# Activation buffers per channel tile, and a plain float32 second matmul in the attention of the last 512 queries

## The chip, the core and the metric

The kernel runs on one core of a Trainium2 chip. The metric is the device time of one execution in microseconds. Five engines matter here: PE (TensorE, matrix multiplication; PEld is its weight load), DVE (VectorE), ACT (ScalarE), POOL (GpSimd) and SP (SyncE, which here only issues DMAs). Each engine runs its own instructions in their order and waits on semaphores for the others. Matmuls write to PSUM, which DVE and ACT read; DMAs move data between memory and SBUF.

## What is computed

A trunk of two layers over 2048 positions of width 1024, all in float32: a gated short convolution, one K/V projection, then a stick-breaking attention with 8 heads of 64, and RMS norms before, between and behind them. Cut to what matters:

```
u = rmsnorm(x) @ w_in_a                       # 1024 -> 4 x 1024: B, C, h, G
x = x + ((B * conv3(C * h)) * silu(G)) @ w_out_a
k, v = split(rmsnorm(x) @ w_kv)               # 8 heads of 64
q, g = split(rmsnorm(x) @ w_in_b)
z = q k^T / 8                                 # strictly causal
rev = reverse cumulative sum over keys of log_sigmoid(-z)
o = exp(z + rev) @ v                          # masked entries are 0
x = x + (o * silu(g)) @ w_out_b
out = rmsnorm(x)
```

## The kernel before

**Layout.** Positions stand in reverse order on the free dimension, so that the cumulative sum over later keys becomes a running product from left to right. The 2048 positions are cut into four chunks of 512 (`c` = 0 to 3); the last, `c` = 3, is "the last 512 queries" and sees all four key chunks. Channels are cut into eight tiles of 128 (`k` = 0 to 7).

**Split operands.** Most matmuls are float32r, a reduced form of float32. To keep precision an operand is split into a high part (ACT's copy to float32r, line 173) and a low part (the source minus the high part, line 174, on DVE or POOL). A linear layer (`mm3`, lines 210 to 222) then takes three matmuls per channel tile: high x high, high x low, low x high.

**Buffers.** `act_tile` (line 115) is one tile of 32 KB per partition that holds the high and low parts of all eight channel tiles of one activation; there are two. They hold `h` (normed input), `y` (mixer output), `xn` (normed residual) and later `og` (gated attention output) in turn. `x1` and, at the end, `x2` share one tile of 16 KB with tag `og`. Weights are split once and kept in memory (`split_d`); their split tiles `whl` rotate through four buffers, the raw ones `wraw` through two. A buffer is given out again when all readers of its last tile are done.

**Folding.** `fold_gains` (line 361) multiplies the norm gains into `w_kv` and `w_in_b`, 16 tiles of 128x1024. Each is loaded to a `wraw` buffer, scaled on DVE (line 366), split into a `whl` buffer (lines 192 and 173 to 174) and stored (line 194). It runs beside the input projections of chunks 0 and 1.

**Attention.** For a head and a query chunk (`attention`, line 465) the key chunks are visited from the diagonal down. For each of four query blocks of 128: two matmuls for the scores `z` (lines 486, 487), two sigmoids on ACT (489, 491), a running product on DVE (500) whose last column is carried to the next key chunk, and a multiplication for the weights `w` (504). Then, for each of four key blocks (`kb` = 3 to 0): transposes of `w` on PE into PSUM tile `wt` (512), a split of `wt` into `wth` on ACT and `wtl` on DVE (519, that is 173 and 174), and two float32r matmuls (521, 522) that add `wth` and `wtl` times v to the accumulator `av`. The 128 columns of the v operand are the high and the low part of 64 channels, so half of the partitions of `av` holds v's high part and the other half its low part; lines 529 and 530 add the halves at the end of a head. On the diagonal, the blocks have 512, 384, 256 and 128 valid queries; the last is padded to 256.

**Order.** Generators yield estimated costs, and `merge` advances the stream that is furthest behind its share; the framework's own scheduler then settles each engine's order. In the last stage the first six heads of chunk 3 are merged with a fill: the rest of chunk 3's projections (`proj_rest`), and the output projections `out_b` and norms of chunks 0 to 2. Heads 6 and 7 are merged with the output projection of chunk 3 over its first 384 channels (`out_b_last`). There, every third matmul of the fill (`GRP`) is tied to follow an anchor, the second `av` matmul of the block `SLACK` = 8 anchors back (lines 217 to 219, 523). After the last head `out_b_last` adds the last 128 channels and writes the norm.

Of the kernel before, what the change touches and what calls it, by code (L numbers as in the profile page):

```python
# [14 lines left out]
P = 128  # L15
S = 2048
D = 1024
NH = 8
# [3 lines left out]
NR, NW, NT, NL, NWB, NRAW, NWTS = 5, 8, 4, 5, 4, 2, 2  # L22
# [8 lines left out]
GRP, GRY, SLACK = 3, 6, 8  # L31
# [14 lines left out]
def kernel(  # L46
# [49 lines left out]
    v_d = [dram.tile([P, 4, NH, 2, 64], F32, name=f"v_d_{c}") for c in range(NCH)]  # L96
    sg_d = [[dram.tile([P, CH], F32, name=f"sg_d_{c}_{h}") for h in range(NH // 2)] for c in range(NCH)]
# [17 lines left out]
    def act_tile(nm):  # L115
        return sb.tile([P, 2, KD, CH], F32R, name=nm, tag="act", bufs=2)
# [59 lines left out]
    def load_raw(src, nm, kt=KD):  # L176
        raw = sb.tile([P, kt, P], F32, name=f"wr_{nm}", tag="wraw", bufs=NRAW)
        if len(src.shape) == 2:
            src = src.rearrange("(k p) n -> p k n", p=P)
        nc.sync.dma_start(out=raw, in_=src)  # L180
        return raw

# [6 lines left out]
    def split_w(raw, key, nm, kt=KD, eng=nc.vector):  # L189

        wt = w_tile(nm, kt)
        split(wt[:, 0], wt[:, 1], raw, eng)
        split_d[key] = dram.tile([P, 2, kt, P], F32, name=f"sw_{nm}")
        nc.sync.dma_start(out=split_d[key], in_=wt.bitcast(F32))
        return wt

    def load_w(src, key, nm, kt=KD, eng=nc.vector):

        if key not in split_d:
            return split_w(load_raw(src, nm, kt), key, nm, kt, eng)  # L200
        wt = w_tile(nm, kt)
        nc.sync.dma_start(out=wt.bitcast(F32), in_=split_d[key])
        return wt
# [6 lines left out]
    def mm3(ps, wts, a, kt=KD):  # L210

        hi, lo = wts[:, 0], wts[:, 1]
        n = 0
        for k in range(kt):
            for w, m in ((hi, 0), (hi, 1), (lo, 0)):
                ins = nc.tensor.matmul(ps, w[:, k, :], a[:, m, k, :], start=n == 0, stop=n == 3 * kt - 1)  # L216
# [16 lines left out]
    def norm_x_late(c, between=None):  # L233

        hc = act_tile(f"h_{c}")
        xs = []
        for k in range(KD):
            if k == 1 and between is not None:
                between()
            tag, bufs = (("w", NW), ("R", NR) if k < NR else ("ld", NL))[c]  # L240
            x = sb.tile([P, CH], F32, name=f"xh_{c}_{k}", tag=tag, bufs=bufs)
            nc.sync.dma_start(out=x, in_=xT[k * P:(k + 1) * P, cols(c)])
            xs.append(x)
            ga = gains["a"][:, k:k + 1]
            nc.scalar.activation(hc[:, 0, k, :], x, AF.Copy, scale=ga)
            nc.vector.scalar_tensor_tensor(out=hc[:, 1, k, :], in0=x, scalar=ga, in1=hc[:, 0, k, :].bitcast(F32),
                                           op0=ALU.mult, op1=ALU.subtract)
        return hc, xs
# [26 lines left out]
    def norm_x(c):  # L275
        hc = act_tile(f"h_{c}")
        pb = bcast(rx[c], f"hb{c}")
        for k in range(KD):
            x = load_x(c, k, "n")
            nc.vector.scalar_tensor_tensor(out=x, in0=x, scalar=gains["a"][:, k:k + 1], in1=pb,  # L280
                                           op0=ALU.mult, op1=ALU.mult)
            split(hc[:, 0, k, :], hc[:, 1, k, :], x)
        return hc
# [88 lines left out]
    def proj_out(c):  # L372

        y = act_tile(f"y_{c}")
        for k in range(KD):
            t = ld512(f"yr_{c}_{k}")
            nc.sync.dma_start(out=t, in_=y_d[c][k])
            split(y[:, 0, k, :], y[:, 1, k, :], t, nc.gpsimd if k in YLP else nc.vector)
        acc = sb.tile([P, CH], F32, name=f"acc_x1{c}", tag="acc", bufs=2)
        yield 0.0  # L380
        for ob in range(KD):
            wts = load_w(w_out_a[0][:, ob * P:(ob + 1) * P], ("o", ob), f"o{c}_{ob}")
            ps = lin(f"po_{c}_{ob}")
            yield from mm3(ps, wts, y)
            if ob == 0:
                x1 = sb.tile([P, KD, CH], F32, name=f"x1_{c}", tag="og", bufs=1)
            x = x1[:, ob, :]
# [5 lines left out]
        xn = act_tile(f"xn_{c}")  # L393
        pb = rstd_bcast(acc, f"x1{c}")
        for k in range(KD):
            t = x1[:, k, :]
            nc.vector.tensor_mul(t, t, pb)
            split(xn[:, 0, k, :], xn[:, 1, k, :], t, nc.gpsimd if k in XNL else nc.vector)
        kept[c] = xn
        yield YP[c] * 24 * MM  # L400
# [21 lines left out]
    def proj_v(c, vb):  # L422
# [10 lines left out]
        nc.sync.dma_start(out=v_d[c][:, :, 2 * vb:2 * vb + 2, :, :], in_=vt.bitcast(F32))  # L433
        yield rest(24) + 2 * MM
# [30 lines left out]
    def attention(c, h, ot):  # L465
# [8 lines left out]
        for kc in range(c, -1, -1):  # L474
# [4 lines left out]
            vt = sb.tile([P, 4, 2, 64], F32R, name=f"vv_{nm}", tag="vv", bufs=2)  # L479
            nc.scalar.dma_start(out=vt.bitcast(F32), in_=v_d[kc][:, :, h, :, :])  # L480
# [26 lines left out]
            for kb in range(3, -1, -1):  # L507
# [5 lines left out]
                first, final = diag and kb == 3, kc == 0 and kb == 0  # L513
                wh = sb.tile([P, CH], F32R, name=f"wth_{nm}_{kb}", tag="wth", bufs=NWTS)
# [8 lines left out]
                anchors.append(ins)  # L523
# [18 lines left out]
    def og_tile(c):  # L542

        if c == 0:
            og_t[0] = sb.tile([P, 2, 4, CH], F32R, name="og_0", tag="og", bufs=1)
        elif c == 1:
            t = act_tile("og_12")
            og_t[1], og_t[2] = t[:, :, 0:4, :], t[:, :, 4:8, :]
        elif c == 3:
            t = act_tile("og_3")  # L550
            og_t[3] = t[:, 0].rearrange("p (m k) n -> p m k n", m=2)
            x2_t.append(sb.tile([P, KD, CH], F32, name="x2_3", tag="og", bufs=1))

    x2_t = []

    def gated(c, k, r=None):

        if c not in og_t:
            og_tile(c)
        og = og_t[c]  # L560
# [8 lines left out]
        split(og[:, 0, k, :], og[:, 1, k, :], r)  # L569
# [51 lines left out]
    def out_b_last(c):  # L621

        og, x2 = og_t[c], x2_t[0]
        for ob in range(KD):
# [4 lines left out]
            nc.sync.dma_start(out=x2[:, ob, :], in_=x1_d[c][ob])  # L629
            nc.vector.tensor_add(x2[:, ob, :], x2[:, ob, :], ps)  # L630
# [8 lines left out]
        for ob in range(KD):  # L639
            ps = lin(f"pol_{ob}")  # L640
            yield from mm3(ps, wl[ob // 4][:, :, ob % 4:ob % 4 + 1, :], og[:, :, 3:4, :], kt=1)
            nc.vector.tensor_add(x2[:, ob, :], x2[:, ob, :], ps)
            if ob < 2:
                nc.scalar.activation(acc[ob], x2[:, ob, :], AF.Square)
            else:
                sq = t512(f"sq_x2{c}{ob}")
                nc.scalar.activation(sq, x2[:, ob, :], AF.Square)
# [9 lines left out]
        for k in range(KD):  # L657
            if k in (1, 4, 7):
                nc.scalar.activation(x2[:, k, :], x2[:, k, :], AF.Copy, scale=gains["f"][:, k:k + 1])
                nc.gpsimd.tensor_mul(x2[:, k, :], x2[:, k, :], pbs)  # L660
            else:
                nc.vector.scalar_tensor_tensor(out=x2[:, k, :], in0=x2[:, k, :], scalar=gains["f"][:, k:k + 1],
                                               in1=pb, op0=ALU.mult, op1=ALU.mult)
            nc.sync.dma_start(out=outT[k * P:(k + 1) * P, cols(c)], in_=x2[:, k, :])
# [101 lines left out]
```

## Time and profile before

| | |
|---|---|
| Median of 3 runs | 1909.34 us (1906.65 to 1910.77) |
| The profiled execution | 1907.57 us, its span 1905.8 us |
| Mean granted TensorE clock in it | 0.977 |
| PE, DVE, ACT, POOL busy | 1784.0, 1264.6, 769.7, 436.2 us |
| Moved by DMA | 443.64 MB, 233 GB/s |
| Attention of chunk 3: first and last head end | 1527.2 and 1874.3 us |

How to read it: the span runs from the first to the last instruction of the profiled execution. A group's row gives line, engine, operation, output <- inputs, shape of array and operands, count, then busy time and mean of one in ns, then the idle time of the engine just before and who ended it. A matmul's duration is a latency; since matmuls are pipelined, two of them in a row start closer together than one lasts. A row of the table of stages gives a window in us and its length, then busy time and (count) of PE, PEld, DVE, ACT and POOL, the granted clock, the DMA share and GB/s.

### The profile page before, as it was taken

What the parts mean: (1) busy time and instruction counts of PE and PEld (TensorE: products, weight loads), DVE (VectorE), ACT (ScalarE), POOL (GpSimd) and SP (SyncE); (2) the same over time, 40 slices, a digit from 0 to 9 for tenths busy, and PEclk for the clock granted to TensorE, in tenths of its full rate; (3) what the DMA queues carried; (4) which work ended last, traced back from release to release, by engine and by line L of the source; (5) the groups of instructions that cost most, each with busy time, mean ns of one, the idle gap of its engine ahead of it and who ended that gap; (6) DMA issues with size and microseconds to landing.
All of it is one profiled execution on the core that took longest, in us unless ns stands there. A gap on an engine that the chain in (4) does not pass through costs nothing.

```text
span 1905.8 us, 24702 instructions
## 1 busy us (share of the span) xinstructions
PE 1784.0 (94%) x8312; PEld 1449.4 (76%) x8312; DVE 1264.6 (66%) x1895; ACT 769.7 (40%) x1481; POOL 436.2 (23%) x822
## 2 busy tenths in 40 slices
PE   7899999999999999999999999999979999878785
PEld 5787777778888888888788888888857788656563
DVE  7644554574334264428888346788897999999996
ACT  6312222241123133314545233444555666565553
POOL 5000000000011021103123112222422224654641
PEclk9999999999999999999999999999999999999897
DMA  9648787798887779776767776655746665877751
GB/s 314 210 150 248 248 254 237 243 312 304 295 284 270 258 237 286 246 262 224 242 211 268 238 253 219 202 175 197 258 144 196 197 199 193 284 225 250 252 177 50
DMA packets 226702, 443.64 MB, mean 233 GB/s; under 512 B 16912, under 2 KB 131600, under 8 KB 199952
## 3 DMA queue, kind: packets, MB, share of 16 engines
q1 hardware_dynamic: 166496, 383.30, 60.0%
q10 hardware_dynamic: 59920, 58.74, 10.9%
q8 instruction: 66, 1.08, 0.2%
q14 instruction: 60, 0.49, 0.1%
q0 software_dynamic: 160, 0.02, 0.1%
HBM read 314.34 MB, written 127.66 MB: 232 GB/s over the span
## 4 chain that ended last, share of the span: by engine, by line
PE 69%; DVE 14%; DMA 9%; issue 4%; ACT 2%; POOL 1%; SPq 0%; ACTq 0%; POOLq 0%; DVEq 0%
PE pX L216 8%; PE po L216 7%; PE pG L216 7%; PE pC L216 7%; PE pB L216 6%; PE pg L216 5%; PE pk L216 5%; PE pq L216 5%; PE pv L216 4%; PE wt L512 4%; DVE R L500 4%; PE av L522 3%; DVE w L504 2%; PE av L521 2%; PE z L486 2%
## 5 line engine op out<-in xcount | busy, mean ns | idle before, releaser
L500 DVE TENSOR_TENSOR_SCAN R<-R,R,ones 128x512 f32<-128x512 f32 x192 | 256.6, 1339 | 11.4 <-ACT R L489 11.1
L489 ACT ACTIVATE R<-z 128x512 f32<-128x512 f32 (+1 forms) x320 | 174.2, 544 | 173.1 <-DVE R L500 78.4
L174 DVE TENSOR_TENSOR wtl<-wt,wth 128x512 fp32r<-128x512 f32 (+1 forms) x320 | 185.6, 600 | 67.2 <-ACT wth L173 66.3
L504 DVE TENSOR_TENSOR w<-w,R 128x512 f32<-128x512 f32 (+1 forms) x320 | 212.2, 671 | 21.3 <-POOL R L499 3.0
L173 ACT CAST wth<-wt 128x512 fp32r<-128x512 f32 (+1 forms) x320 | 160.3, 526 | 160.1 <-PE wt L512 137.4
L216 PE MATMUL pC<-h,whl_C 128*128 128x512 f32 x768 | 197.1, 405 | 14.4 <-ACT whl_C L173 8.3
L216 PE MATMUL pG<-h,whl_G 128*128 128x512 f32 x768 | 186.6, 393 | 9.9 <-ACT whl_G L173 9.9
L499 POOL COPY R<-R 128x1 f32<-128x1 f32 x192 | 112.3, 585 | 360.8 <-DVE R L500 293.3
L216 PE MATMUL pX<-h,whl_X 128*128 128x512 f32 x768 | 187.6, 393 | 6.0 <-ACT cs L320 3.9
L216 PE MATMUL po<-y,whl_o 128*128 128x512 f32 x768 | 187.8, 394 | 2.0 <-DVE x L389 1.3
L512 PE MATMUL wt<-ident,w 128*128 128x128 f32 x1088 | 177.8, 278 | 9.2 <-DVE w L504 5.1
L216 PEld LDWEIGHTS pC<-h,whl_C 128*128 128x128 f32 x768 | 148.2, 195 | 49.4 <-ACT whl_C L173 8.3
L216 PE MATMUL pB<-h,whl_B 128*128 128x512 f32 x768 | 185.6, 392 | 0.0
L216 PEld LDWEIGHTS pG<-h,whl_G 128*128 128x128 f32 x768 | 143.2, 188 | 41.0 <-ACT whl_G L173 11.6
L491 ACT ACTIVATE w<-z 128x512 f32<-128x512 f32 (+1 forms) x320 | 172.7, 543 | 0.5 <-PE wt L512 0.5
L216 PEld LDWEIGHTS pX<-h,whl_X 128*128 128x128 f32 x768 | 142.2, 188 | 37.6 <-ACT cs L320 5.1
L216 PEld LDWEIGHTS po<-y,whl_o 128*128 128x128 f32 x768 | 144.2, 189 | 33.5 <-DVE x L389 1.9
L512 PEld LDWEIGHTS wt<-ident,w 128*128 128x128 f32 x1088 | 138.6, 143 | 38.3 <-DVE w L504 7.2
L216 PEld LDWEIGHTS pB<-h,whl_B 128*128 128x128 f32 x768 | 143.0, 188 | 30.1 <-DVE cv L356 0.4
L522 PE MATMUL av<-wtl,vv 128*128 128x512 f32 (+1 forms) x320 | 129.1, 405 | 36.7 <-DVE wtl L174 36.6
L500 DVE TENSOR_TENSOR_SCAN R<-R,ones 128x512 f32<-128x512 f32 (+3 forms) x128 | 116.1, 913 | 33.8 <-POOL R L495 32.2
L486 PE MATMUL z<-kt,q 128*128 128x512 f32 (+1 forms) x320 | 129.1, 405 | 4.1 <-ACT w L491 3.4
(170 smaller groups left out, 2655.3 us busy)
## 6 DMA issues: line engine op xcount, KB each, us to landing
whl_o<-sw_o SPq DMA_DIRECT2D x24, 1024.0 KB, 5.7
kt<-k_d ACTq DMA_DIRECT2D x80, 256.0 KB, 3.6
vv<-v_d ACTq DMA_DIRECT2D x80, 256.0 KB, 4.0
whl_C<-sw_C SPq DMA_DIRECT2D x16, 1024.0 KB, 5.4
whl_X<-sw_X SPq DMA_DIRECT2D x16, 1024.0 KB, 5.5
whl_B<-sw_B SPq DMA_DIRECT2D x16, 1024.0 KB, 5.5
whl_G<-sw_G SPq DMA_DIRECT2D x16, 1024.0 KB, 5.2
whl_k<-sw_kv SPq DMA_DIRECT2D x16, 1024.0 KB, 5.2
```

The lines of the kernel that those rows point to most:

```text
L173: nc.scalar.copy(hi, src)
L174: eng.tensor_sub(lo, src, hi.bitcast(F32))
L216: ins = nc.tensor.matmul(ps, w[:, k, :], a[:, m, k, :], start=n == 0, stop=n == 3 * kt - 1)
L486: nc.tensor.matmul(ps[:, lom:CH], q2[:, 0, qi * P:(qi + 1) * P], kt[:, lom:CH], start=True, stop=False)
L489: nc.scalar.activation(R[:, lo + 1:CH + 1], ps[:, lo:CH], AF.Sigmoid, scale=-0.125)
L491: nc.scalar.activation(w[:, lo:CH], ps[:, lo:CH], AF.Sigmoid, scale=0.125)
L499: nc.gpsimd.tensor_copy(R[:, 0:1], carry[qi])
L500: nc.vector.tensor_tensor_scan(out=R[:, lo + 1:CH + 1], data0=R[:, lo + 1:CH + 1], data1=ones[:, 0:1].to_broadcast([P, CH - lo]), initial= ...
L504: nc.vector.tensor_mul(w[:, lo:CH], w[:, lo:CH], R[:, lo:CH])
L512: nc.tensor.transpose(wt[:, qi * P:(qi + 1) * P], ws[qi][:, kb * P:(kb + 1) * P], ident)
L521: nc.tensor.matmul(av[:, 0:n], vs, wh[:, 0:n], start=first, stop=False)
L522: ins = nc.tensor.matmul(av[:, 0:n], vs, wl[:, 0:n], start=False, stop=final)
```

## The change

**Buffers.** `act_tile` now gives one channel tile (4 KB per partition: high and low part of 512 positions) out of 16 buffers, and `h`, `y`, `xn` and `og` are lists of such tiles. `x1` and `x2` are lists of eight 2 KB tiles with tag `og`. The memory is the same; a tile comes free when its own readers are done. `og` moves to the `act` buffers.

**Folding** takes half a weight tile at a time, 128x512, in two of the 2 KB buffers, and no longer passes through `wraw` and `whl`: per tile of 128x1024 there are two loads, two scalings, two splits and four stores.

**v twice.** `proj_v` also stores an unsplit float32 copy of v (`vf_d`), made by one more ACT copy.

**The second matmul.** For chunk 3's heads (`plain=True`), `wt` is copied once by ACT to a float32 tile; nothing is split on DVE. Two key blocks are collected, and then two plain float32 matmuls with 64 columns of v each are issued: the first block (3 or 1) to partitions 0 to 63 of `av`, the second (2 or 0) to partitions 64 to 127. Lines 529 and 530 add the halves as before. On the diagonal the second block (384 queries) is filled with zeros to 512 columns by POOL. Anchors stand at every second block, in the other chunks too, and `SLACK` is 4.

```diff
-GRP, GRY, SLACK = 3, 6, 8
+GRP, GRY, SLACK = 3, 6, 4
...
-    def act_tile(nm):
-        return sb.tile([P, 2, KD, CH], F32R, name=nm, tag="act", bufs=2)
+    def act_tile(nm, k):
+
+        return sb.tile([P, 2, CH], F32R, name=f"{nm}_{k}", tag="act", bufs=NA)
...
-                raw = load_raw(src[:, i * P:(i + 1) * P], f"fold_{nm}{i}")
-                nc.vector.tensor_mul(raw, raw, gain.unsqueeze(2).to_broadcast([P, KD, P]))
-                split_w(raw, (nm, i), f"{nm}{i}")
+                split_d[nm, i] = dram.tile([P, 2, KD, P], F32, name=f"sw_{nm}{i}")
+                for j in range(0, KD, 4):
+                    hi, lo = (sb.tile([P, 4, P], F32R, name=f"fold{m}_{nm}{i}_{j}", tag="og", bufs=KD) for m in range(2))
+                    raw = lo.bitcast(F32)
+                    nc.sync.dma_start(out=raw, in_=src[j * P:(j + 4) * P, i * P:(i + 1) * P].rearrange("(k p) n -> p k n", p=P))
+                    nc.vector.tensor_mul(raw, raw, gain[:, j:j + 4].unsqueeze(2).to_broadcast([P, 4, P]))
+                    split(hi, lo, raw)
+                    for m, t in enumerate((hi, lo)):
+                        nc.sync.dma_start(out=split_d[nm, i][:, m, j:j + 4, :], in_=t.bitcast(F32))
...
+        vf = sb.tile([P, 4, 2, 64], F32, name=f"vf_{c}_{vb}", tag="t", bufs=NT)
+        nc.scalar.copy(vf, pt.rearrange("p (b h d) -> p b h d", b=4, d=64))
+        nc.sync.dma_start(out=vf_d[c][:, :, 2 * vb:2 * vb + 2, :], in_=vf)
...
+            if plain:
+                vt = sb.tile([P, 4, 64], F32, name=f"vv_{nm}", tag="vv", bufs=2)
+                nc.scalar.dma_start(out=vt, in_=vf_d[kc][:, :, h, :])
+            else:
...
+                if plain:
+                    ws_ = sb.tile([P, CH], F32, name=f"wts_{nm}_{kb}", tag=("wth", "wtl")[kb % 2], bufs=NWTS)
+                    nc.scalar.copy(ws_[:, 0:nq * P], wt[:, 0:nq * P])
+                    if diag and kb == 2:
+
+                        nc.gpsimd.memset(ws_[:, 3 * P:CH], 0.0)
+                    two.append((ws_, CH if diag and kb == 2 else nq * P))
+                    if kb % 2 == 0:
+                        for half, (ws_, m) in enumerate(two):
+                            ins = nc.tensor.matmul(av[half * 64:(half + 1) * 64, 0:m], vt[:, kb + 1 - half, :], ws_[:, 0:m],
+                                                   start=diag and kb == 2, stop=kc == 0 and kb == 0)
+                        two.clear()
+                        anchors.append(ins)
+                    if kb:
+                        yield (1900.0 if diag else 3500.0) / 4
+                    continue
...
-                anchors.append(ins)
+                if kb % 2 == 0:
+                    anchors.append(ins)
...
-            yield from attention(c, 2 * hb, ot)
-            yield from attention(c, 2 * hb + 1, ot)
+            yield from attention(c, 2 * hb, ot, True)
+            yield from attention(c, 2 * hb + 1, ot, True)
```

More of the change, by code (lines that the diff above doesn't have):

```diff
@@ L96 @@
     v_d = [dram.tile([P, 4, NH, 2, 64], F32, name=f"v_d_{c}") for c in range(NCH)]
+    vf_d = [dram.tile([P, 4, NH, 64], F32, name=f"vf_d_{c}") for c in range(NCH)]
     sg_d = [[dram.tile([P, CH], F32, name=f"sg_d_{c}_{h}") for h in range(NH // 2)] for c in range(NCH)]
@@ L174, in split @@
         eng.tensor_sub(lo, src, hi.bitcast(F32))
[L176 to L181, printed above, removed]
     def w_tile(nm, kt=KD):
@@ L187 @@
     split_d = {}
[L189 to L195, printed above, removed]
     def load_w(src, key, nm, kt=KD, eng=nc.vector):
         if key not in split_d:
-            return split_w(load_raw(src, nm, kt), key, nm, kt, eng)
+            wt = w_tile(nm, kt)
+            raw = sb.tile([P, kt, P], F32, name=f"wr_{nm}", tag="wraw", bufs=NRAW)
+            nc.sync.dma_start(out=raw, in_=src.rearrange("(k p) n -> p k n", p=P))
+            split(wt[:, 0], wt[:, 1], raw, eng)
+            split_d[key] = dram.tile([P, 2, kt, P], F32, name=f"sw_{nm}")
+            nc.sync.dma_start(out=split_d[key], in_=wt.bitcast(F32))
+            return wt
         wt = w_tile(nm, kt)
@@ L215, in mm3 @@
             for w, m in ((hi, 0), (hi, 1), (lo, 0)):
-                ins = nc.tensor.matmul(ps, w[:, k, :], a[:, m, k, :], start=n == 0, stop=n == 3 * kt - 1)
+                ins = nc.tensor.matmul(ps, w[:, k, :], a[k][:, m, :], start=n == 0, stop=n == 3 * kt - 1)
                 if fine[1] and len(anchors) > SLACK and n % GRP == 0:
@@ L244, in norm_x_late @@
             ga = gains["a"][:, k:k + 1]
-            nc.scalar.activation(hc[:, 0, k, :], x, AF.Copy, scale=ga)
-            nc.vector.scalar_tensor_tensor(out=hc[:, 1, k, :], in0=x, scalar=ga, in1=hc[:, 0, k, :].bitcast(F32),
+            hk = act_tile(f"h_{c}", k)
+            nc.scalar.activation(hk[:, 0, :], x, AF.Copy, scale=ga)
+            nc.vector.scalar_tensor_tensor(out=hk[:, 1, :], in0=x, scalar=ga, in1=hk[:, 0, :].bitcast(F32),
                                            op0=ALU.mult, op1=ALU.subtract)
+            hc.append(hk)
         return hc, xs
@@ L462, in proj_rest, with attention @@
             yield from proj_g(c, i)
-    def attention(c, h, ot):
+    def attention(c, h, ot, plain=False):
         hb, hi_ = divmod(h, 2)
@@ L478, in attention @@
             nc.scalar.dma_start(out=kt.bitcast(F32), in_=k_d[kc][h])
-            vt = sb.tile([P, 4, 2, 64], F32R, name=f"vv_{nm}", tag="vv", bufs=2)
-            nc.scalar.dma_start(out=vt.bitcast(F32), in_=v_d[kc][:, :, h, :, :])
+            if plain:
+                vt = sb.tile([P, 4, 64], F32, name=f"vv_{nm}", tag="vv", bufs=2)
+                nc.scalar.dma_start(out=vt, in_=vf_d[kc][:, :, h, :])
+            else:
+                vt = sb.tile([P, 4, 2, 64], F32R, name=f"vv_{nm}", tag="vv", bufs=2)
+                nc.scalar.dma_start(out=vt.bitcast(F32), in_=v_d[kc][:, :, h, :, :])
+            two = []
             ws = []
@@ L540 @@
     og_t = {}
[L542 to L554, printed above, removed]
     def gated(c, k, r=None):
-        if c not in og_t:
-            og_tile(c)
-        og = og_t[c]
+        og = act_tile(f"og_{c}", k)
+        og_t.setdefault(c, []).append(og)
         sg = ld512(f"sga_{c}_{k}")
@@ L621, in out_b_last @@
     def out_b_last(c):
-        og, x2 = og_t[c], x2_t[0]
+        og = og_t[c]
+        x2 = [sb.tile([P, CH], F32, name=f"x2_{c}_{k}", tag="og", bufs=KD) for k in range(KD)]
         for ob in range(KD):
@@ L628, in out_b_last @@
             yield from mm3(ps, wts, og, kt=3)
-            nc.sync.dma_start(out=x2[:, ob, :], in_=x1_d[c][ob])
-            nc.vector.tensor_add(x2[:, ob, :], x2[:, ob, :], ps)
+            nc.sync.dma_start(out=x2[ob], in_=x1_d[c][ob])
+            nc.vector.tensor_add(x2[ob], x2[ob], ps)
             yield rest(9)
```

49 lines of the change are left out of this document (25 added, 24 removed).

## The prediction

> **What bounds the kernel now.** I read the page first: the busy line of each engine, the rows of slices, the chain. Then a table of stages: the first 400 us (input projections of chunks 0 and 1, with the folding of the gains), 400 to 1400, the passage to the last chunk, and the attention of the last 512 queries, cut where its third and sixth head end and where its last one ends.
>
> ```profile
> span 1905.8 us, 24702 instructions
> PE 1784.0 (94%) x8312; PEld 1449.4 (76%) x8312; DVE 1264.6 (66%) x1895; ACT 769.7 (40%) x1481; POOL 436.2 (23%) x822
> DVE  7644554574334264428888346788897999999996
> PEclk9999999999999999999999999999999999999897
> ```
> ```profile
> core 0: us, PE busy (x) PEld busy (x) DVE busy (x) ACT busy (x) POOL busy (x), PEclk, DMA share, GB/s
> 0.00:400.00 400.00, 367.49 (x1572) 296.85 (x1573) 220.40 (x315) 117.46 (x159) 42.74 (x62) 0.98 0.76 238
> 400.00:1400.00 1000.00, 995.85 (x4762) 827.35 (x4761) 587.94 (x918) 359.76 (x745) 183.28 (x449) 1.00 0.75 249
> 1400.00:1486.00 86.00, 70.79 (x339) 54.07 (x338) 73.88 (x123) 47.66 (x97) 22.07 (x48) 0.96 0.52 168
> 1486.00:1617.00 131.00, 128.16 (x660) 105.16 (x661) 122.41 (x161) 83.46 (x169) 42.60 (x83) 1.00 0.59 192
> 1617.00:1777.00 160.00, 132.55 (x609) 101.42 (x607) 153.68 (x214) 97.44 (x193) 94.26 (x119) 0.94 0.78 255
> 1777.00:1875.00 98.00, 77.75 (x342) 57.27 (x342) 89.08 (x130) 54.30 (x105) 45.00 (x57) 0.90 0.55 171
> ```
>
> The page's 94% for PE hides two regimes. From 400 to 1400 PE is 99.6% busy: nothing that relieves another engine is worth anything there. From 1617 to 1875 DVE is busy 242.8 of 258 us (94%) and PE shows holes. Between them, 1486 to 1617, both are full (128.2 and 122.4 of 131). Who waits for whom in 1486 to 1875 says the same:
>
> ```profile
> ACT R L489 <- DVE R L500: 42.4, 38, 3.4
> PEld av L522 <- DVE wtl L174: 39.8, 37, 4.0
> PE av L522 <- DVE wtl L174: 27.7, 27, 3.6
> ```
>
> PE's largest wait is for the low half of a weight block, the subtraction (line 174) which this change takes away.
>
> **The change part by part: what DVE loses.** In the last chunk each key block of 128 has one such subtraction. Its rows for heads 0 to 5 (1486 to 1777), then heads 6 and 7 (1777 to 1875):
>
> ```profile
> L174 DVE TENSOR_TENSOR wtl<-wt,wth 128x512 fp32r<-128x512 f32 x78 | 51.6, 677 | 4.0 <-ACT wth L173 4.0
> L174 DVE TENSOR_TENSOR wtl<-wt,wth 128x384 fp32r<-128x384 f32 x6 | 3.3, 548 | 0.1
> L174 DVE TENSOR_TENSOR wtl<-wt,wth 128x256 fp32r<-128x256 f32 x6 | 2.4, 404 | 0.0
> L174 DVE TENSOR_TENSOR wtl<-wt,wth 128x128 fp32r<-128x128 f32 x6 | 1.7, 276 | 0.0
> L174 DVE TENSOR_TENSOR wtl<-wt,wth 128x512 fp32r<-128x512 f32 x26 | 17.6, 681 | 3.1 <-ACT wth L173 3.1
> ```
>
> That is 59.0 us of DVE in the first window; for two heads a third of the short ones (2.5) and 17.6 make 20.1. ACT's copy out of PSUM stays one for one. DVE keeps 122.4 + 153.7 - 59.0 = 217.1 us in the first window; at the share it holds now (276.1 of 291, 0.949) it needs 229 us. In the second it keeps 69.0; at its share now (0.909) that is 76 us. These are floors set by DVE.
>
> **What PE holds.** The same first window, by kind:
>
> ```profile
> L216 PE MATMUL pob<-og,whl_ob 128*128 128x512 f32 x252 | 70.3, 416 | 2.9 <-DVE x1o L591 2.6 <-DVE og L174 0.3
> L512 PE MATMUL wt<-ident,w 128*128 128x128 f32 x345 | 56.8, 280 | 1.2 <-DVE wtl L174 0.8 <-DVE w L504 0.3
> L486 PE MATMUL z<-kt,q 128*128 128x512 f32 x79 | 35.0, 444 | 1.3 <-ACT w L491 1.2
> L522 PE MATMUL av<-wtl,vv 128*128 128x512 f32 x78 | 34.8, 446 | 15.9 <-DVE wtl L174 15.8
> L521 PE MATMUL av<-wth,vv 128*128 128x512 f32 x78 | 33.4, 428 | 6.5 <-DVE ot L530 5.0 <-ACT wth L173 1.5
> L487 PE MATMUL z<-kt,q 128*128 128x512 f32 x79 | 31.5, 399 | 0.0
> L216 PE MATMUL pg<-xn,whl_gg 128*128 128x512 f32 x96 | 25.9, 400 | 0.0
> L216 PE MATMUL pv<-xn,whl_v 128*128 128x512 f32 x60 | 16.3, 404 | 0.0
> L216 PE MATMUL pk<-xn,whl_k 128*128 128x512 f32 x48 | 13.0, 398 | 0.0
> L216 PE MATMUL pq<-xn,whl_q 128*128 128x512 f32 x48 | 12.9, 395 | 0.0
> ```
>
> The mean of a row is a latency; matmuls overlap, so their price is the distance of starts. It comes from runs in the timeline (start, length of the run), with a mean of one to take off its end:
>
> ```profile
> 172.36 5.60 PE L216 MATMUL pB<-h,whl_B 128*128 128x512 f32 x24
> 1702.25 0.60 PE L512 MATMUL wt<-ident,w 128*128 128x128 f32 x4
> 1702.61 0.42 PE L486 MATMUL z<-kt,q 128*128 128x384 f32 x1
> L216 PE MATMUL pB<-h,whl_B 128*128 128x512 f32 x768 | 185.6, 392 | 0.0
> L125 PE MATMUL pst_x<-ones,acc_x 128*128 128x1 f32 x64 | 9.4, 266 | 3.2 <-DVE acc_x L651 3.2
> ```
>
> A float32r matmul of 512 columns: (5.60 - 0.39) / 23 = 0.2265 us. Four transposes hold PE from 1702.25 to 1702.61: 0.09 each; within the run they start (0.60 - 0.28) / 3 = 0.107 apart. The first window has 660 + 609 = 1269 records: 818 of 512 columns (185.3 us), 345 transposes (31.1), and 106 short ones which I put at 0.12 (12.7), 229 us in all, 79% of 291. The second, at the same mean of 0.18 per record, has 342 x 0.18 = 62 us. How full can both engines be? In 1486 to 1617, 660 x 0.18 = 119 us of PE work and 122.4 us of DVE fit in 131: 0.91 and 0.93. With DVE near 80% afterwards I take 0.95 for PE; it may be 0.92 to 0.98, worth 8 us either way.
>
> **What a plain float32 matmul costs.** No row has one of 512 columns, none on half the columns. Two rows bound it. The single column sums of line 125 are plain float32: 8 calls of 4 matmuls make 32, and 64 records stand there, so one is issued as two. If a record costs what float32r costs, a matmul is 2 x 0.2265 = 0.453. The transposes, the other float32 work, start 0.107 apart for 128 columns, where float32r's rate gives 0.057: twice. Then one is 4 x 0.2265 = 0.906. I take the second, the nearer in column count.
>
> A pair of key blocks costs 4 x 0.2265 = 0.906 now. It becomes two matmuls: 0.906 if the halves of the array work fully side by side, 1.812 if one after the other. I take the middle, 1.359: with starts in program order the first block's second record and the second block's first can share time, the outer two can't. A row of 392 ns with starts 226 apart also has 0.165 us of overlap, which matmuls on different shapes of the array may not share; a pair has two such changes, and I charge one, 0.165 (none to two).
>
> The Trainium skill, TensorEngine Tiling (Array Packing), Key Properties, speaks against the change: a change of the tiling mode drains the engine. By that rule both overlaps are lost and the forecast becomes 1865. No row of this trace has a second shape, so it can't say.
>
> Per head: six full pairs gain 0.453 each (2.72); the diagonal's first pair goes from 2 x 0.2265 + 2 x 0.17 = 0.79 to 1.36 (+0.57), its second from 0.45 to 0.57 (+0.11); eight changes add 1.3. That is +4.7 us: 28 us in the first window, 9.4 in the second. First window: (229 + 28) / 0.95 = 271 us, over DVE's 229, so PE becomes the bound: 291 - 271 = 20 saved. Second: PE 71 / 0.95 = 75, DVE 76: DVE stays the bound, just, and 22 are saved.
>
> **Folding the gains.** It moves from the ring of four weight tiles to the per-tile buffers. What the ring costs now:
>
> ```profile
> L216 PE MATMUL pG<-h,whl_G 128*128 128x512 f32 x768 | 186.6, 393 | 9.9 <-ACT whl_G L173 9.9
> 174.51 0.32 SPq L194 DMA_DIRECT2D sw_kv<-whl_kv  x1
> 179.62 1.04 ACT L173 CAST whl_G<-wr_G 128x1024 fp32r<-128x1024 f32 x1 [3.05 <-DMA sw_kv<-whl_kv]
> ```
>
> A folded tile must land in memory before the next weight's cast may take its slot, and PE stands still: 9.9 us. I take 9.9 off. Against it: 32 DMA issues become 96 on SP's queue, at 0.32 us 20 us more; a store there still waits for DVE's subtraction with later weight loads behind it. So the bounds are -14 and +10. The work on DVE is the same bytes in twice the instructions, and in 0 to 400 DVE is 55% busy: nothing.
>
> **Edits at nothing.** Sixteen activation tiles for two large ones release earlier; PE idles 4 us from 400 to 1400, so 0 to -4. The added plain copy of v is one ACT copy of a 512-column PSUM tile and one store per v projection, 16 in all; ACT is 36% busy where they lie, and uncovered they cost what the present copy of the same tile costs, 9.4 us:
>
> ```profile
> L427 ACT COPY vT<-pv 128x512 f32<-128x512 f32 x16 | 9.4, 587 | 41.3 <-PE pv L216 41.2
> ```
>
> The v loads halve in bytes on the same queue. Pacing: an anchor per pair and a slack of four pairs is the old distance of eight blocks.
>
> **Sum.** The profiled execution took 1907.57 us, its span 1905.8; the median shown is 1909.34, 1.8 more, inside the spread of its runs. 1907.6 - 9.9 - 20 - 22 = 1855.
>
> **The rivals.** *Fully side by side* (0.20): a pair stays at 0.906, a head gains 1.4 us, the first window is (229 + 8.4) / 0.95 = 250: 1907.6 - 9.9 - 41 - 22 = 1835. For it: separate columns, separate outputs. Against it: program order. The Trainium skill, TensorE: Matmul & The Clock Gate, Part 3, says that matmuls in separate column tiles run concurrently; no run here shows it.
>
> *One after the other* (0.25): the halves aren't used at once, and the change doesn't do what it says. A head gains 8.0 us; the first window is (229 + 48) / 0.95 = 292, no gain, the second (62 + 16) / 0.95 = 82: 1882. For it: no row shows two matmuls overlapping by more than their tail.
>
> *Slower* (0.08): one after the other, and the weights of each record are not loaded under the matmul before.
>
> ```profile
> L216 PEld LDWEIGHTS pB<-h,whl_B 128*128 128x128 f32 x768 | 143.0, 188 | 30.1 <-DVE cv L356 0.4
> 172.14 5.40 PEld L216 LDWEIGHTS pB<-h,whl_B 128*128 128x128 f32 x24
> ```
>
> The place is the pair; the price 4 x 0.19 (the first row) and the second overlap, 7.5 us more per head: (229 + 93) / 0.95 = 339 and 97: 1945. It decides where PE's work in both windows, (229 + 62 + 8 heads' extra) / 0.95, reaches 291 + 98 + 9.9 us, what they and folding take now: 11 us extra per head, a pair at 0.906 + 11 / 8 = 2.3 us. Against it: the second row's 24 loads run beside the 24 matmuls quoted above (172.36 to 177.96) and add nothing.
>
> *Nothing left* (0.05): one after the other with both overlaps lost (+11) and no gain from folding (+10): 1903, too close to tell.
>
> **How the numbers follow.** The forecast holds 0.42, its own range 1845 to 1866. A measurement of this kernel tells 0.2%, 3.8 us, from no change. Faster: 0.42 + 0.20 + 0.25 = 0.87; same 0.05; slower 0.08. The range reaches from 1826 (side by side, with folding's better bound and PE at 0.97) to 1893 (one after the other, with folding's worse bound).
>
> **What would show it.** Right: no subtraction to wtl in the last chunk, DVE's total down by about 79, less the few that folding's doubled instructions cost; 256 records of the second matmul in the last chunk under a shape other than 128*128, a pair holding PE for about 1.4 us; pG's wait for whl_G gone; PE busy over 95% up to the sixth head's end. Wrong: pairs at 0.9 or 1.8 us or more, new waits of weight loads in the first 400 us, or DVE still over 90% busy with PE idle.

## The result, and the profile after

The changed kernel takes 1900.36 us (median of 10 runs, 1892.03 to 1903.37), the kernel before 1909.57 (10 runs, 1903.99 to 1912.43): a ratio of 0.9949 [0.9935, 0.9964]. It is faster, by 9.2 us where 54 were forecast, and outside the range. The head of its page:

```profile
span 1901.3 us, 24847 instructions
PE 1825.6 (96%) x8312; PEld 1414.4 (74%) x8312; DVE 1202.0 (63%) x1799; ACT 782.3 (41%) x1513; POOL 445.8 (23%) x814
DVE  7866533564233273538885517878897666888785
PEclk9999999999999999999999999999999999999898
...
L210 PE MATMUL pG<-h,whl_G 128*128 128x512 f32 x768 | 185.4, 391 | 0.0
...
L535 PE MATMUL av<-wts,vv 128*64 128x512 f32 (+2 forms) x256 | 118.5, 606 | 5.9 <-ACT wts L528 5.2
```

DVE lost 62.6 us of busy time. PE gained 41.6 with the same number of records. The idle time ahead of `pG` (last column) is 0.0 where it was 9.9. The stages, cut as in the prediction, at 400 and 1400 us and where heads 2, 5 and 7 of chunk 3 end:

```profile
core 0: us, PE busy (x) PEld busy (x) DVE busy (x) ACT busy (x) POOL busy (x), PEclk, DMA share, GB/s
0.00:400.00 400.00, 378.74 (x1632) 308.61 (x1633) 234.38 (x373) 128.38 (x186) 46.72 (x62) 0.98 0.79 256
400.00:1400.00 1000.00, 993.57 (x4760) 825.00 (x4759) 590.49 (x934) 371.01 (x768) 185.53 (x457) 1.00 0.75 247
1469.00:1620.00 151.00, 150.11 (x650) 93.90 (x649) 98.59 (x113) 86.17 (x173) 46.97 (x81) 1.00 0.51 163
1620.00:1777.00 157.00, 146.82 (x616) 87.17 (x615) 127.69 (x166) 94.48 (x189) 95.39 (x114) 0.97 0.77 240
1777.00:1871.00 94.00, 86.78 (x346) 47.09 (x344) 75.96 (x99) 54.71 (x107) 46.84 (x54) 0.96 0.53 160
```

The last stage starts 17 us earlier (1469 for 1486). Then heads 0 to 5 take 308 us where they took 291 and 271 were forecast; heads 6 and 7 take 94 where they took 98 and 76 were forecast. So the gain of the first 400 us is there, and the attention, for which the change to the matmul was costed at 42 us of gain, lost 13. The waits of 1469 to 1871:

```profile
PEld wt L524 <- issue: 82.1, 106, 1.6
ACT wts L528 <- PE wt L524: 46.4, 43, 2.7
DVE R L512 <- ACT R L501: 42.3, 33, 3.0
```

PE no longer waits for a low half. DVE now waits for ACT, ACT for PE's transposes, and the transposes' weight loads start 106 times some 0.8 us late with no releaser in the profile ("issue"). Each of these 106 stands behind a record of the second matmul, as the timeline shows (start, length of the run of records, one row each; the last row is a weight load):

```profile
1470.67 1.08 PE L535 MATMUL av<-wts,vv 128*64 128x512 f32 x4 [0.68 <-DVE ot L559]
1471.68 1.40 PE L210 MATMUL pv<-xn,whl_v 128*128 128x512 f32 x5
1501.35 1.07 PE L535 MATMUL av<-wts,vv 128*64 128x512 f32 x2
1502.35 0.66 PE L524 MATMUL wt<-ident,w 128*128 128x128 f32 x4
1502.94 1.07 PE L535 MATMUL av<-wts,vv 128*64 128x512 f32 x2
1503.94 0.66 PE L524 MATMUL wt<-ident,w 128*128 128x128 f32 x4
1502.35 0.42 PEld L524 LDWEIGHTS wt<-ident,w 128*128 128x128 f32 x4 [0.81 <-issue]
```

The second matmul is two records, as forecast. At 1470.67 the four records of a pair stand together and are over in 1.01 us: single records start 7, 473 and 7 ns apart, so the two column halves do run side by side. At 1501.35 only one matmul of the pair is there; it takes 1.00 us alone, four transposes follow, and its partner takes another 1.00. In the compiled order of PE 49 of the 64 pairs are parted like this; the first matmul needs only its own copy, which is likely why, but no run shows the scheduler's reason. The 42 of them that are of full size cost 2.0 us and use half the array at a time.

### The profile page after: what moved, and what is told of

It reads as the page before. It is cut to its first block, busy times and chain, and to the rows that moved or that the text cites. A ratio compares the mean times of both kernels' runs of the same rounds, so it can differ in the third digit from the quotient of the medians.

```text
span 1901.3 us, 24847 instructions
## 1 busy us (share of the span) xinstructions
PE 1825.6 (96%) x8312; PEld 1414.4 (74%) x8312; DVE 1202.0 (63%) x1799; ACT 782.3 (41%) x1513; POOL 445.8 (23%) x814
## 3 DMA queue, kind: packets, MB, share of 16 engines
q8 instruction: 66, 1.08, 0.2%
## 4 chain that ended last, share of the span: by engine, by line
PE 75%; DVE 10%; DMA 6%; issue 4%; POOL 2%; ACT 1%; SPq 0%; POOLq 0%; ACTq 0%; DVEq 0%
PE po L210 8%; PE pX L210 8%; PE pB L210 8%; PE pC L210 7%; PE pG L210 7%; PE wt L524 5%; PE pg L210 5%; PE pk L210 4%; PE pq L210 4%; PE pv L210 4%; PE av L535 4%; DVE R L512 3%; PE z L498 2%; PE z L499 2%; DVE w L516 2%
## 5 line engine op out<-in xcount | busy, mean ns | idle before, releaser
L516 DVE TENSOR_TENSOR w<-w,R 128x512 f32<-128x512 f32 (+2 forms) x320 | 210.9, 668 | 24.6 <-POOL R L511 2.4
L524 PEld LDWEIGHTS wt<-ident,w 128*128 128x128 f32 x1088 | 128.8, 141 | 107.6 <-issue 82.2
L210 PE MATMUL pC<-h,whl_C 128*128 128x512 f32 x768 | 192.8, 399 | 13.7 <-ACT whl_C L176 7.9
L177 DVE TENSOR_TENSOR wtl<-wt,wth 128x512 fp32r<-128x512 f32 x192 | 107.3, 582 | 50.0 <-ACT wth L176 49.3
L176 ACT CAST wth<-wt 128x512 fp32r<-128x512 f32 x192 | 92.3, 511 | 99.1 <-PE wt L524 91.7
L535 PE MATMUL av<-wts,vv 128*64 128x512 f32 (+2 forms) x256 | 118.5, 606 | 5.9 <-ACT wts L528 5.2
```

The source lines that it names most:

```text
L176: nc.scalar.copy(hi, src)
L177: eng.tensor_sub(lo, src, hi.bitcast(F32))
L210: ins = nc.tensor.matmul(ps, w[:, k, :], a[k][:, m, :], start=n == 0, stop=n == 3 * kt - 1)
L516: nc.vector.tensor_mul(w[:, lo:CH], w[:, lo:CH], R[:, lo:CH])
L524: nc.tensor.transpose(wt[:, qi * P:(qi + 1) * P], ws[qi][:, kb * P:(kb + 1) * P], ident)
L535: ins = nc.tensor.matmul(av[half * 64:(half + 1) * 64, 0:m], vt[:, kb + 1 - half, :], ws_[:, 0:m], start=diag and kb == 2, stop=kc == 0 an ...
```

## The experiments

The theory after this result: the halves work side by side, but the order parts them, and that is what the attention lost. The first rival: the matmul isn't the matter; DVE's relief was worth little to begin with. The experiments were run in several rounds, in which the kernel before had medians of 1904.5 to 1911.2 us; a ratio is to the kernel before in the same round, and a few us between two rounds tell nothing.

**The pairs together.** The changed kernel, with ordering edges on PE that keep the next transposes behind a pair and a pair behind the transposes of its second block; 52 of 64 pairs are then adjacent. Nothing is left out.

```diff
+                    if plain and pair:
+                        tc.add_manual_dep(tr.ins, pair[-1].ins.name, PACE, reason="pair")
...
+                            if half == 0:
+                                tc.add_manual_dep(ins.ins, tr.ins.name, PACE, reason="pair")
+                        pair.append(ins)
```

> The changed kernel with compile-time ordering edges on PE only: the first matmul of a pair after the second block's transposes, the next block's transposes after the pair's second matmul. Compiled order: 52 of the 64 pairs have nothing between their two matmuls, against 15 in the changed kernel. Theory A (order): the two halves run side by side only when the two matmuls are adjacent on PE, a pair then takes 1.0 us instead of 2.0, 37 more pairs save 37 us of PE in a stage where PE is the bound: 1863 to 1872. Theory B (chain): the last stage waits on the chain sigmoid, scan, copy and not on PE, so shorter pairs leave PE idle: 1890 to 1900. Theory C (buffers): the loss in the last stage comes from the per-tile buffers, nothing changes: 1897 to 1903.

**Both matmuls on one half.** The same, with both matmuls of a pair on partitions 0 to 63; the addition of the halves at the end of a head is left out.

```diff
-                            ins = nc.tensor.matmul(av[half * 64:(half + 1) * 64, 0:m], vt[:, kb + 1 - half, :], ws_[:, 0:m],
+                            ins = nc.tensor.matmul(av[0:64, 0:m], vt[:, kb + 1 - half, :], ws_[:, 0:m],
...
```

> As e1, but both matmuls of a pair write to partitions 0 to 63, so that they use the same column half; the addition of the two halves at the end of a head is left out, since one half holds the sum. Theory A: the pair takes 2.0 us although adjacent, and the time goes back to about that of the changed kernel, 1895 to 1910. If adjacency helps for another reason (fewer changes of shape, transposes no longer in between), it stays near e1, within 10 us.

Together: 1883.57 us (1881.93 to 1885.26), 0.9879 [0.9864, 0.9894], between the two expectations: 17 us better than the change as it was (13 by the ratios). On one half: 1906.16 (1903.99 to 1910.05), 1.0 [0.999, 1.001], 22.6 us more than together. The timelines of the two:

```profile
1490.29 0.39 PE L500 MATMUL z<-kt,q 128*128 128x512 f32 x1
1490.52 0.39 PE L501 MATMUL z<-kt,q 128*128 128x512 f32 x1
1490.83 1.08 PE L539 MATMUL av<-wts,vv 128*64 128x512 f32 x4
1491.84 1.09 PE L526 MATMUL wt<-ident,w 128*128 128x128 f32 x8
```
```profile
1491.42 1.93 PE L539 MATMUL av<-wts,vv 128*64 128x512 f32 x4
```

The same four records last 1.08 us on two halves and 1.93 on one. So the halves pay, once the order lets them. But 17 us is half of what the better price should bring: 37 more pairs are adjacent (52 less 15), 31 of full size at 1 us and 6 short ones of the diagonal at 0.36 (0.58 for 0.94), 33 us in all. Heads 0 to 2 and 3 to 7 of the pairs together say where the rest went:

```profile
1466.00:1601.00 135.00, 133.56 (x657) 91.87 (x656) 98.44 (x113) 84.98 (x172) 45.43 (x81) 1.00 0.58 182
1601.00:1849.00 248.00, 221.38 (x955) 132.98 (x953) 207.10 (x263) 150.15 (x296) 142.69 (x168) 0.96 0.68 213
```

In heads 0 to 2, where PE is full, 17 more pairs are adjacent (22 of 24, where 5 were), and 16 us came: 135 for 151. In heads 3 to 7, 20 more are adjacent (30 of 40, where 10 were), and 3 us came: 248 for 251.

Being neighbours is not enough there. Of the 26 adjacent pairs of full size, 10 start their second half 0.3 to 0.5 us after the first; of the 19 in heads 0 to 2 one does, by 0.1. One of the 10, with the weight load of its second half, which waits for ACT's copy of the second block:

```profile
1840.93 1.56 PE L539 MATMUL av<-wts,vv 128*64 128x512 f32 x4 [0.29 <-ACT wts L532]
1841.42 0.19 PEld L539 LDWEIGHTS av<-wts,vv 128*64 128x64 f32 x2 [0.30 <-ACT wts L532]
```

From start to next start, the second matmuls take 15.0 us less of PE than in the change as it was in heads 0 to 2, and 11.8 less in heads 3 to 7. Of these 11.8 only 3 shorten the stage, so there something else holds as well.

**The parts alone.** The changed kernel with the split second matmul (buffers and folding alone); the kernel before with the plain matmul alone; and the first of these with folding back in the rings. The second has the extra copy of v too, and the anchors of the change.

```diff
-            yield from attention(c, 2 * hb, ot, True)
-            yield from attention(c, 2 * hb + 1, ot, True)
+            yield from attention(c, 2 * hb, ot)
+            yield from attention(c, 2 * hb + 1, ot)
```

> The changed kernel with the split second matmul back in the last chunk's heads; buffers, folding, anchors and the extra copy of v stay. Theories A and B: the head start of 17 us before the last chunk's attention stays and the last stage takes what it took before: 1888 to 1896. Theory C: the buffers cost the last stage some 13 us, so little is left: 1899 to 1906.

> The kernel before with the plain second matmul and the extra copy of v, old buffers and old folding. Theory A: the last stage gets PE-bound and longer by some 13 us, 1915 to 1925; pairs are 1.0 us adjacent and 2.0 apart. Theory B: about equal to before, 1905 to 1912. Theory C: faster than before by tens of us, 1870 to 1890.

For the third, in addition:

```diff
+                raw = sb.tile([P, KD, P], F32, name=f"wr_fold_{nm}{i}", tag="wraw", bufs=NRAW)
...
+                wt = w_tile(f"{nm}{i}")
+                split(wt[:, 0], wt[:, 1], raw)
...
-                for j in range(0, KD, 4):
...
+                nc.sync.dma_start(out=split_d[nm, i], in_=wt.bitcast(F32))
```

> As e2, with the folding of the gains back in the rings of raw and split weight tiles; per-tile activation buffers stay. Theory F (folding carries the gain of the buffers): back by 10 us or more, 1894 to 1906. Theory T (the release per tile carries it): 1884 to 1890. Both in part: in between.

Buffers and folding alone: 1884.02 (1881.94 to 1889.88), 0.9878 [0.9861, 0.9895], 4 us below the lowest time expected. The plain matmul alone: 1918.58 (1909.74 to 1920.56), 1.0054 [1.0036, 1.0072], slower. With folding in the rings: 1908.02 (1904.53 to 1910.4), 0.9999 [0.9989, 1.0008], 2 us above what the first theory expected. So folding in the new way carries 24 us, the buffers per channel tile and the extra copy of v together nothing that shows without it, and the matmul costs 11.8. (The new folding lives in the new buffers, so it was not timed without them.) The parts add up: -22.7 + 11.8 = -10.9, measured -9.2. PE's waits in 100 to 400 us, folding in the rings and then not:

```profile
PE pG L210 <- ACT whl_G L176: 9.8, 4, 2.6
PE pX L210 <- ACT cs L316: 2.9, 3, 1.5
PE pX L210 <- DVE cv L352: 2.0, 2, 1.4
```
```profile
PE pX L210 <- DVE cv L352: 3.6, 3, 1.2
```

And the same 300 us by engine, in the same order:

```profile
100.00:400.00 300.00, 285.39 (x1234) 232.73 (x1234) 154.63 (x196) 72.34 (x88) 13.35 (x28) 0.99 0.76 235
```
```profile
100.00:400.00 300.00, 296.40 (x1305) 244.49 (x1304) 162.78 (x235) 77.95 (x108) 14.63 (x28) 1.00 0.76 247
```

PE does 71 records more in the same time; at 0.2265 us that is 16 us, of which 11 are waits (14.7 less 3.6); the granted clock, 0.99 and then 1.00 over 300 us, is some 3 of the rest. Over the first 400 us it is 74 records (1654 for 1580), 17 of the 19 us by which these two profiled executions differ.

**DVE relieved, PE as it was.** Buffers and folding alone, with the subtraction of the low part left out in chunk 3; both matmuls read the high part, and the low part's buffers serve it too.

```diff
-                split(wh[:, 0:nq * P], wl[:, 0:nq * P], wt[:, 0:nq * P])
...
+                if c == 3:
+                    nc.scalar.copy(wh[:, 0:nq * P], wt[:, 0:nq * P])
+                    wl = wh
```

> As e2 (split second matmul), but in the last chunk DVE's subtraction is left out and both matmuls of a block read the high part: the low part of the weights is left out of the result, PE does the same work as in e2, DVE 79 us less. Theory A (DVE was the bound, as the prediction had it, and the plain matmul's pairs eat the gain): 40 us or more under e2, 1835 to 1848. Theory B (the stage is bound by the order of the work and the chain across engines, DVE's share of 94% being waiting that others fill): within 12 us of e2, 1872 to 1884.

1868.46 (1864.61 to 1872.14), 0.979 [0.9773, 0.9808]: 15.6 us for the relief that the forecast priced at 42, with no dearer matmul in the way. It lies between the ranges of the two theories. Heads 0 to 2 and 3 to 7, with the subtraction and then without:

```profile
1469.00:1602.00 133.00, 129.56 (x669) 106.57 (x668) 123.08 (x164) 86.53 (x176) 38.98 (x86) 1.00 0.63 198
1602.00:1857.00 255.00, 208.66 (x945) 159.42 (x943) 239.33 (x340) 148.63 (x292) 137.43 (x173) 0.91 0.69 216
```
```profile
1467.00:1594.00 127.00, 126.10 (x657) 104.84 (x656) 98.96 (x112) 85.03 (x173) 44.07 (x81) 1.00 0.64 207
1594.00:1839.00 245.00, 207.91 (x953) 160.01 (x951) 204.17 (x263) 148.65 (x294) 140.39 (x169) 0.91 0.72 225
```

In heads 0 to 2 PE was full before (97%) and is full after (99%): DVE's 24 us bring 6. In heads 3 to 7 DVE's 35 us bring 10, and then neither engine is full (PE 85%, DVE 83%).

**The fill lighter, later, earlier, freer.** All four start from the pairs together. Lighter: in the last stage the two correcting matmuls of all channel tiles but the first and the last are left out, 268 matmuls. Later and earlier: the exponent by which the planner lets the fill follow the progress of heads 0 to 5, at 1.5 and 0.75 (shown). Freer: the fill may run eight pairs ahead, not four.

```diff
+                if not (fine[1] and m + (w is lo) and 0 < k < kt - 1):
...
-    merge((fill, TR + 3 * TO), (heads(0, 3, 3), 0.75 * ta(3)))
+    merge((fill, TR + 3 * TO), (heads(0, 3, 3), 0.75 * ta(3), 0.75))
...
-GRP, GRY, SLACK = 3, 6, 4
+GRP, GRY, SLACK = 3, 6, 8
```

> As e1, but in the last stage the linear layers leave out the two correcting matmuls of all channel tiles but the first and the last: 268 matmuls of 512 columns fewer, 61 us of PE, and DVE's and ACT's work unchanged. Theory A (PE is the bound once the pairs are together): 35 us or more under e1, below 1850. Theory B (chain): less than 15 us, above 1868.

> As e1, with the fill of the first six heads advanced as the heads' share of progress to the power 1.5 instead of in step, so that PE has less fill beside heads 0 to 2 and more beside heads 3 to 5. Theory A (PE is the bound beside heads 0 to 2 in e1, 98.5% busy there, and has holes later): 8 to 20 us under e1, 1864 to 1876. Theory B (chain): within 5 us of e1.

> The kernel of the pairs together, with the other chunks' work put earlier beside heads 0 to 5 (exponent 0.75 in place of 1 in the planner). Later cost 15 us. Theory A (the stage wants PE's work beside the early heads, so that less of it waits behind the last ones): 3 to 8 us faster, 1875 to 1881. Theory B (the even mixture is already the best, and every shift costs): 1884 to 1895.

> The kernel of the pairs together, with 8 second matmuls in place of 4 that the other chunks' matmuls may run ahead of the attention. Theory A (the written order between attention and the other work holds the engines back): 2 to 8 us faster, 1876 to 1882. Theory B (the buffers and the serial steps of the attention hold them): 1881 to 1890, no change.

Lighter: 1853.68 (1851.59 to 1857.8), 0.9716 [0.9699, 0.9732], 30 us for 61 us of matmuls (268 at 0.2265), between the two expectations: 19 in heads 0 to 2, where 136 records are gone, and 10 in heads 3 to 7, where 106 are. Later: 1898.73 (1894.33 to 1900.11), 0.9943 [0.9928, 0.9958], a loss that neither theory had. Earlier: 1894.65 (1893.04 to 1897.47), 0.9944 [0.9927, 0.9961]. Freer: 1883.51 (1881.12 to 1888.7), 0.9887 [0.9866, 0.9908], no change, though heads 6 and 7 took 14 us less and heads 0 to 5 11 more. Neither shift of the mixture helps; the order's slack moves time between heads and not out of the stage.

**The split matmul in heads 0 to 2, the plain one in 3 to 7.** PE is full in the first three heads, so there the cheaper matmul should count, and in the later heads DVE's relief. The pairs stay together; nothing is left out.

```diff
-            yield from attention(c, 2 * hb, ot, True)
-            yield from attention(c, 2 * hb + 1, ot, True)
+            yield from attention(c, 2 * hb, ot, hb > 1)
+            yield from attention(c, 2 * hb + 1, ot, hb > 0)
```

> The kernel of the pairs together, with the plain second matmul in heads 3 to 7 alone; heads 0 to 2 have the split one again. Beside the pairs together (1883.6) theory A (beside heads 0 to 2 PE is nearly all busy, so the dearer second matmul is paid there in full, and DVE's copies and subtractions cost nothing): 24 pairs at 0.906 us in place of 1.010 and 12 of the 64 that stood apart: 3 to 8 us faster, 1875 to 1881. Theory B (what counts is how the engines' orders fit together, not one engine's load): between 1880 and 1890, no gain.

1875.92 (1873.06 to 1877.44), 0.9839 [0.9819, 0.9859]: 7.7 us better than the pairs together, as the first theory had it, and the fastest version here that computes everything: by the ratios to before, 1.1% ahead of the change.

**What holds heads 3 to 7.** From this version, one run leaves out GpSimd's part of the output norms of chunks 0 to 2 (the sums of squares behind the first channel tile, and the multiplications by the norm); two others have five and six `R` tiles, with the load ring cut to four tiles in both to make room.

```diff
-            square_into(acc_b[c], x, ob == 0, f"x2{c}{ob}", nc.gpsimd)
+            if ob == 0:
+                square_into(acc_b[c], x, True, f"x2{c}{ob}", nc.gpsimd)
+            else:
+                sq = t512(f"sq_x2{c}{ob}")
+                nc.scalar.activation(sq, x, AF.Square)
...
-            nc.gpsimd.tensor_mul(t, t, pbs)
```

> The kernel with the split matmul in heads 0 to 2 and the plain one in heads 3 to 7 (1875.9), with GpSimd's part of the other chunks' output norms left out: the additions of the squares and the multiplications by the norm, 21 + 24 instructions and 69 us of GpSimd in the last stage. Theory A (in heads 3 to 7 VectorE's instructions with two operands are held up by GpSimd's, so part of its busy time is standing): the mean of the multiplication of the weights in heads 3 to 5 falls from 1004 ns to under 800, and the time to 1855 to 1867. Theory B (GpSimd's work lies in time that VectorE has free): the mean falls too, but the time stays at 1870 to 1878.

> The same base with four load tiles in place of five, the comparison for the next kernel. Both theories: 1874 to 1885.

> As the kernel before it, with six R tiles in place of five. Theory A (ScalarE's sigmoid waits for VectorE to give back an R tile, and this ties the engines together): 4 to 10 us faster than the kernel with five. Theory B (the ring follows VectorE, it does not hold it): within 3 us.

Without GpSimd's part: 1862.22 (1857.95 to 1864.5), 0.9743 [0.9722, 0.9764], 14 us less (18 by the ratios). Five tiles: 1877.66 (1869.95 to 1878.69), 0.9815 [0.9785, 0.9844]; six: 1884.2 (1882.39 to 1889.08), 0.9865 [0.9843, 0.9887], 6.5 us more than five, which neither theory had and nothing here explains. So a longer ring of `R` doesn't help. Heads 3 to 7, and in heads 3 to 5 the multiplication of the weights, with GpSimd's part and without it; the wait is PE's for that multiplication in heads 3 to 7:

```profile
1600.00:1846.00 246.00, 221.19 (x945) 131.69 (x943) 203.33 (x260) 148.06 (x292) 139.69 (x167) 0.95 0.69 214
```
```profile
L518 DVE TENSOR_TENSOR w<-w,R 128x512 f32<-128x512 f32 x38 | 38.1, 1004 | 6.0 <-POOL R L513 2.4
```
```profile
PE wt L526 <- DVE w L518: 12.8, 6, 4.2
```
```profile
1601.00:1829.00 228.00, 212.69 (x940) 129.24 (x938) 176.65 (x256) 146.59 (x292) 69.35 (x122) 0.99 0.72 230
```
```profile
L518 DVE TENSOR_TENSOR w<-w,R 128x512 f32<-128x512 f32 x38 | 30.9, 814 | 4.4 <-ACT w L505 0.8 <-POOL w L509 0.5
```
```profile
PE wt L526 <- DVE w L518: 0.2, 1, 0.2
```

These heads are 18 us shorter. DVE is busy 27 us less with the same instructions (four short ones, 1.2 us, fall outside the second window). PE's 12.8 us of waiting for the multiplication are gone; other waits grew, and PE stands idle 15.3 us instead of 24.8. The granted clock rises from 0.95 to 0.99. DVE's own idle time that GpSimd ends did not shrink (10.7 us with GpSimd's part, 15.0 without), so the gain is not an earlier result of GpSimd. The mean of the multiplication fell to 814 ns, not below 800 as expected.

The Trainium skill, SBUF — State Buffer, "SBUF: two separate sides", says that a VectorE operation with two SBUF inputs and a GpSimd operation that reads SBUF exclude each other for a whole instruction. These rows agree. In heads 3 to 5 with GpSimd's part, 6 of the 38 multiplications overlap no GpSimd instruction of over 0.3 us, and 15 overlap only its copy of one column: both have a mean of 0.69 us. The 17 that overlap a GpSimd operation on a tile of 128x512 have a mean of 1.39, five of them over 1.7. The kernel before shows it, too: the same multiplication in heads 0 to 2, and then in 3 to 5, where POOL is busy more than twice as long:

```profile
L504 DVE TENSOR_TENSOR w<-w,R 128x512 f32<-128x512 f32 x39 | 27.5, 705 | 4.3
L504 DVE TENSOR_TENSOR w<-w,R 128x512 f32<-128x512 f32 x39 | 38.2, 984 | 2.0
```

## Why the prediction was wrong, step by step

**"These are floors set by DVE."** This step failed, and with it the 42 us of the last stage. It read DVE's 94% in heads 3 to 7 as work, and divided the rest by a share. The run without the low part tests it with PE's work unchanged: 15.6 us came, not 42. By the forecast's rule the 99.0 and 204.2 us that DVE kept there, at its shares with the subtraction (0.93 and 0.94), would have taken 107 and 218 us; heads 0 to 2 took 127 and heads 3 to 7 245. First, the forecast pooled heads 0 to 5 into one window of 291 us, (229 + 28) / 0.95, as if PE's work could be spread over it. In heads 0 to 2 PE was full before the change, so DVE's relief there was worth little, and the dearer matmul cost its full price: 151 us for 131, where the second matmuls take 40.0 us from start to start and took 20 by the forecast's prices. The two runs with and without adjacent pairs say the same: there 16 us came when the second matmuls shrank by 15.0, and later 3 when they shrank by 11.8. Moving the fill later cost 15 us, moving it earlier 11. Second, in heads 3 to 7 part of DVE's busy time is standing beside GpSimd, which the removed subtraction doesn't take with it; the run without GpSimd's part made these heads 18 us shorter, and the forecast had no term for GpSimd at all. Its table had the numbers: POOL busy 42.6 us in heads 0 to 2 and 94.3 in 3 to 5.

The floors themselves were mis-sized, too. The rows of the subtraction sum to 79 us, but DVE's records overlap: from 1486 to 1875 us 401 of its 502 start before the one ahead has ended, by a median of 78 ns. So the attention lost 63 us of DVE's busy time (365.2 to 302.2), and DVE kept 226.3 and 76.0 us where 217.1 and 69.0 were forecast.

What the second reason is worth was shown on the version with the split matmul in heads 0 to 2. How much of the 35 us that DVE lost in heads 3 to 7, and that gave 10, goes to GpSimd and how much to the serial steps of a block wasn't tried apart, and stays open.

**"I take the middle, 1.359", and 0.165 for one lost overlap.** Mis-sized, and for the wrong reason. The rate was right: 4 x 0.2265 = 0.906 was forecast for one plain matmul, 1.00 measured. But in the changed kernel a full pair has no middle price. Adjacent it is 1.01 (12 of 14), parted 2.01 (42), and the forecast's sentence "with starts in program order" took the program's order for the engine's: the scheduler sets PE's order, and it parted 49 of 64. "One after the other" was right for those, and "fully side by side" for the others. The forecast's picture, in which the first block's second record and the second block's first share time, is there in 5 pairs of the run with the pairs together, at some 1.5 us, but because a copy comes late, as in the rows shown there.

**The drain.** The charge of one overlap lost in two changes, 0.165, was near. In the run with the pairs together 62 matmuls on column halves start a median of 0.32 us behind a full one of 512 columns, where full ones start 0.227 apart: 0.10. What the way back costs depends on the step that counts as undisturbed. The next matmul starts 0.523 us after the last record. The first record of a pair is followed by the next of its half after 0.480; by that step the way back costs 0.04. In the run with both matmuls on one half the second and third steps of a pair are 0.43; by that step the first record costs 0.05 more, and the way back 0.09. So a pair's two changes cost 0.14 to 0.24 us. By the rule of the Trainium skill, TensorEngine Tiling (Array Packing), Key Properties, as the prediction used it, both overlaps would be lost, 0.33; the runs show less. That column tiles run concurrently, which the prediction cited from the Trainium skill, TensorE: Matmul & The Clock Gate, Part 3, these runs do show: 7 ns between the starts.

**Folding, 9.9 us, bounds -14 and +10.** Right in its place and too small: 24.0 us, outside its bounds. The waits of pG were the largest part, but not the only one. pX's waits shrank from 4.9 to 3.6, and the clock rose. Some 17 us stand in the first 400 us of the profiled executions; where the rest comes from stays open. The 64 more DMA issues on SP's queue cost nothing that shows.

**Edits at nothing.** Right: with folding back in the rings the kernel is at 0.9999 of the kernel before, buffers per channel tile and the copy of v included.

**The rivals.** "Fully side by side" was put at 1835 and "one after the other" at 1882. The runs that come nearest to each gave 1883.6 and 1906.2, 49 and 24 us above, although folding gave 14 more than both assumed. What they share with the forecast is the step of DVE's floors.

**What would show it.** The 256 records under 128*64 are there, pG's wait is gone, and PE is over 95% busy in heads 0 to 5 (296.9 of 308). The pair at 1.4 us is not. DVE's total fell by 62.6, not by 79: up to the last stage it is the same (882.2 us before, 882.5 after), and in the attention 79 us of rows were 63 of busy time. That heads 0 to 2 would get longer with PE full was not among the signs, though the table of stages had PE at 128.2 of 131 there.

## What to carry to other kernels

Here two matmuls on column halves shared the array only where they were neighbours in PE's compiled order and both inputs were ready, so look at that order, not at the program's, and tie the pair together. Rows of one engine can overlap, so the sum of a group's durations is not what its removal takes off the busy time. A relief of an engine is worth what the windows give in which it is the last to be ready: cut windows where the mix of engines changes, and ask of a high busy share whether the instructions last longer there than elsewhere. When a change has two parts, time each alone: here one gained 24 us and the other lost 12, and the best version used the plain matmul only where PE had room.

## What the runs showed of the hardware

A plain float32 matmul of 512 columns on 64 columns of the array is two records, 0.48 and 0.52 us to the next start. With a second one behind it on the same half, the steps between are 0.43. Two of them on the two column halves start 7 ns apart and end in 1.01 us together. Going to the half shape and coming back cost 0.14 to 0.24 us per pair. In the changed kernel the weight load of the next transposes began only when the plain records ahead were over, 106 times with 0.8 us of idle time on average. The multiplication of two SBUF operands on VectorE had a mean of 0.69 us alone or beside GpSimd's copy of one column and 1.39 beside GpSimd's operations on tiles of 128x512, and all of it counts as busy.
